# Operands on 64 byte addresses, one transfer for the Toeplitz matrices, and another fill in the state space stage

## The chip, the cores and the metric

The kernel runs on one core of a Trainium2 chip. The metric is device time in microseconds (us) of one execution, as the median of several. The kernel before takes 1503.35 us, median of 3 runs from 1501.92 to 1510.48.

## The reference

Two transformer blocks run one after the other on 512 tokens of width 1024, in float32. The change touches only a part of the first block, the state space branch (S5), and around it the order in which the projections of that block are worked off.

```python
h = rmsnorm(x, norm_mix_pre[l])
proj = h @ w_in[l]
q, k, v, u, g_attn, g_ssm = jnp.split(proj, splits, axis=-1)
y_attn = sliding_window_attention(q, k, v, sinks[l], rel_bias) @ w_attn_branch[l]
z = jax.nn.gelu(s5_ssm(u, ...))
...
# s5_ssm: 32 groups of 16 channels, one complex diagonal state of 64 entries each
mag = jnp.exp(lr * dt)
ab = mag * (cos(li * dt) + i sin(li * dt))
bb = (ab - 1) / lam * b              # discretized input matrix
h_t = ab * h_(t-1) + bb @ u_t        # along the 512 tokens
y_t = re(c @ h_t) + d_skip * u_t
```

Behind it come the gated merge, the output projection and an MLP, and then the second block (a gated linear recurrence in two directions, attention with a band, a gated feed-forward part).

## The kernel before, in words

Every large matrix product is done in three products of a split operand: `xh*wh`, `xl*wh` and `xh*wl`, where `h` is the operand rounded to the fast float32 form and `l` the rest (`mm3`, lines 217 to 219 of the profile). A weight tile `raw`, 128 x 1024, comes in by a DMA issued by SyncE (L190); ScalarE rounds it to `wh` (L202) and VectorE takes the difference `wl` (L203).

The state space branch is computed in chunks of 8 tokens, 64 chunks (`NCH`). `ssm_prep` makes the constants: from `lam` it takes `mag`, sine and cosine (`sincos`), the powers `pw` of the diagonal state matrix, the tables `ph` of the rotations (products of `un`, the sines and cosines of doubled angles), and the input matrix `bb`. All this is small work of VectorE, 32 to 512 elements wide, in the first 60 us beside the projection that makes `u`.

`ssm_quarter` is a generator that does 8 of the 32 groups (a quarter) in five steps:

1. `rotations` (four products and two sums 128x512 on VectorE), and `combine` for `X` and `L1`, the operands that carry a chunk's input into the state and the state into the output. The load of `U` (the inputs) and the zeros for `kscr` are issued.
2. `xTp`: eight transposes of `X`, copied out by ScalarE into `B8`.
3. `kps`: matmuls of 16 columns and 112 columns with `c0` and `L1`; the result `kev` holds the kernel of a chunk. It is written to the DRAM scratch `kscr` behind a strip of zeros, and read back shifted into `dr`, so that each partition has one row of a Toeplitz matrix. ScalarE copies it in another order of its axes into `D8`, the tile that the profile calls D.
4. `pv`: states of each chunk, two copies of halves between partitions by ScalarE (the tiles `g`), a scan along the chunks, and the products with `rot`.
5. `py`: eight pairs of matmuls, `U` with D8 (the profile's `px` of L789) and `rot` with `L1` (L790), and the result's transfer to DRAM.

TensorE's program order is written by hand. In the state space stage a string `SSM` sets it: `qN` advances quarter N by one step, a number gives so many units of fill, each one `mm3`. The fill (`Feed`) is the projections of k, v and q and then the gates; what it doesn't use up is used in the attention that follows (`G1` and `GZ` say how many of them stand where). The order on the other engines is set by a scheduler, which sees the program and its own times.

The pool of tiles on the left side of the SBUF starts with constants. A tile `even` of 4 bytes per partition in it moves the addresses of what comes after it.

Of the kernel before, what the change touches and what calls it, by code (L numbers as in the profile page):

```python
# [9 lines left out]
F32 = mybir.dt.float32  # L10
# [8 lines left out]
P = 128  # L19
T = 512  # L20
# [36 lines left out]
G1 = 19  # L57
# [23 lines left out]
SSM = 'q0 20 q0 q1 12 q0 3 q0 12 q0 q1 q2 10 q1 3 q1 12 q1 q2 q3 10 q2 3 q2 12 q2 q3 8 q3 3 q3 12 q3'  # L81
# [7 lines left out]
L1E = 0  # L89
# [6 lines left out]
GZ = 4  # L96
# [9 lines left out]
def bc(ap, axis, n):  # L106
    dims = [list(d) for d in ap.ap]
    dims.insert(axis, [0, n])
    return bass.AP(ap.tensor, ap.offset, dims)
# [40 lines left out]
class Net:  # L150
    def __init__(self, tc, a, out, ctx):
        self.tc, self.nc, self.a, self.out, self.ctx = tc, tc.nc, a, out, ctx
        E = ctx.enter_context
        self.const = E(tc.tile_pool(name="const", bufs=1))
        self.wraw = E(tc.tile_pool(name="wraw", bufs=3))
        self.wsp = E(tc.tile_pool(name="wsp", bufs=3))
        self.xn = E(tc.tile_pool(name="xn", bufs=KD))
        self.tmp = E(tc.tile_pool(name="tmp", bufs=5))
        self.sm = E(tc.tile_pool(name="sm", bufs=3))
        self.stk = E(tc.tile_pool(name="stk", bufs=1))  # L160
        self.pmm = E(tc.tile_pool(name="pmm", bufs=3, space=PSUM))
        self.pmx = E(tc.tile_pool(name="pmx", bufs=1, space=PSUM))
        self.pss = E(tc.tile_pool(name="pss", bufs=2, space=PSUM))
        self.pst = E(tc.tile_pool(name="pst", bufs=2, space=PSUM))
        self.dram = E(tc.tile_pool(name="dram", bufs=1, space=DRAM))

        E(tc.tile_pool(name="edge", bufs=1, side="right")).tile([P, 8], F32, name="edge")
        self.sm.tile([P, 1], F32, name="even", bufs=1)
        self.wmode, self.wn, self.after = ("av",), 0, None
        self.deferred, self.fin = [], {}  # L170
# [363 lines left out]
    def sincos(self, pool, s, c, hs, x, n):  # L534

        v = self.nc.vector
        k, y, y2, hc = [pool.tile([P, n], F32, name=f"sc{i}") for i in range(4)]
# [44 lines left out]
    def ssm_prep(self, sp, tp, lam):  # L582
# [4 lines left out]
        dt, e1, th, mag, em1, sn, cs, hs = (N(x) for x in ("dt", "e1", "th", "mag", "em1", "sn", "cs", "hs"))  # L587
# [4 lines left out]
        self.sincos(tp, sn, cs, hs, th, G)  # L592
# [42 lines left out]
        un = [tp.tile([P, 9, G], F32, name=f"un{i}") for i in range(2)]  # L635
        ua, ub = (tp.tile([P, 2, G, 4], F32, name=x) for x in ("ua", "ub"))
        v.tensor_copy(un[0][:, 0, :], cs)
        v.tensor_scalar(un[1][:, 0, :], sn, self.sgn, -1.0, MUL, MUL)
        for j in range(8):
            x, y = [w[:, j, :] for w in un], [w[:, j + 1, :] for w in un]  # L640
            v.tensor_tensor(ta, x[1], x[1], MUL)
            v.tensor_tensor(tb, x[0], x[0], MUL)
            v.scalar_tensor_tensor(y[1], x[0], 2.0, x[1], MUL, MUL)
            v.tensor_tensor(y[0], tb, ta, SUB)
        gp.memset(self.ph[0][:, :, :, 0:1], 1.0)
        gp.memset(self.ph[1][:, :, :, 0:1], 0.0)
        for j in range(3):
            n = 1 << j
            y = [bc(w[:, 3 + j::3, :], 3, n) for w in un]
            self.cmul(v, [w[:, :, :, n:2 * n] for w in self.ph], [w[:, :, :, 0:n] for w in self.ph], y,  # L650
                      [w[:, :, :, 0:n] for w in (ua, ub)])
# [23 lines left out]
        zt = sp.tile([P, 112], F32, name="zt")  # L675
        gp.memset(zt, 0.0)
        self.kscr = [self.dram.tile([8, 16, 240], F32, name=f"kscr{q}") for q in range(4)]
# [29 lines left out]
    def ssm_quarter(self, sp, q):  # L707
# [7 lines left out]
        nc.sync.dma_start(self.kscr[q].rearrange("g c l -> (g c) l")[:, 0:112], self.zt)  # L715
# [10 lines left out]
        def combine(eng, o, x1, w1, x2, w2, op):  # L726
            for h in range(0, 8, 4):
                hs = slice(h, h + 4)
                t = (self.t() if eng is v else sp.tile([P, T], F32, name="gt")).rearrange("p (g c l) -> p g c l", g=4, c=16)
                eng.tensor_tensor(o[:, hs], chan(x1)[:, hs], w1[:, hs], MUL)  # L730
                eng.tensor_tensor(t, chan(x2)[:, hs], w2[:, hs], MUL)
                eng.tensor_tensor(o[:, hs], o[:, hs], t, op)

        combine(v, X, self.bb[:, gs, :], pws(self.ar, 0), self.bbs[:, gs, :], pws(self.ais, 0), ADD)
        combine((v, gp)[L1E], L1, c12[1], pws(self.ain, 1), c12[0], pws(self.ars, 1), SUB)

# [8 lines left out]
        kev = sp.tile([16, 8, P], F32, tag="kd", name="kev")  # L745
        for g4 in range(0, 8, 4):
# [7 lines left out]
            p3 = ps[0:16, :].rearrange("p (g n) -> p g n", g=4)  # L754
            v.tensor_tensor(kev[:, g4:g4 + 4, 0:16], p3[:, :, 0:16], self.dd[:, 8 * q + g4:8 * q + g4 + 4, :], ADD)
            nc.scalar.copy(kev[:, g4:g4 + 4, 16:P], p3[:, :, 16:P])
        nc.sync.dma_start(self.kscr[q][:, :, 112:240].rearrange("g c l -> c g l"), kev)
        dr = sp.tile([P, 8, P], F32, tag="kd", name="dr")
        for i in range(8):
            nc.sync.dma_start(dr[i:P:8, :, :], self.kscr[q][:, :, i * 16:i * 16 + P].rearrange("g c l -> c g l"))  # L760
        D8 = sp.tile([P, 8, 16, 8], F32, name="D8", bufs=DB)
        nc.scalar.copy(D8.rearrange("p g c j -> p g j c"), dr.rearrange("p g (j c) -> p g j c", j=8))
# [923 lines left out]
```

## Time and profile before

| what | value |
| --- | --- |
| median of 3 runs | 1503.35 us |
| the profiled execution | 1509.53 us |
| its span | 1507.8 us |
| TensorE busy (PE) | 1446.4 us, 96% |
| VectorE busy (DVE) | 954.2 us, 63% |
| ScalarE busy (ACT) | 667.8 us, 44% |
| GpSimd busy (POOL) | 225.8 us, 15% |
| DMA traffic | 162.03 MB, 107 GB/s on average |

A busy time is the sum of an engine's instructions, without the time in which it waits. TensorE's matmuls overlap, and their ends are modelled. The granted clock (PEclk) is the share of TensorE's full clock that it was given; 0.50 is the lower of its two levels. A timeline gives a start and a duration for each instruction; the spacing of starts tells what an instruction costs in a row of them, since the durations overlap. The stages meant here are the start (to about 57 us), the state space stage (57 to 204), and the attention of the first block with what follows it.

### The profile page before, as it was taken

How to read it: one execution, taken by the hardware profiler on the slowest of the kernel's cores; microseconds unless marked ns; L12 is line 12 of the kernel's file. 1: busy time of each engine (PE TensorE's matmuls, PEld its weight loads, DVE VectorE, ACT ScalarE, POOL GpSimd, SP SyncE). 2: the span in 40 equal slices, each digit the busy share in tenths (PEclk: the TensorE clock that was granted, in tenths of full speed). 3: DMA queues.
4: the chain of work that ended last, by engine and by line, in shares of the span. 5: the costliest groups of instructions: out<-in, count | busy, mean ns of one | idle time of the engine just before them, and what ended most of it. 6: DMA issues, size and time to landing. Idle time of an engine off the chain costs nothing.

```text
span 1507.8 us, 18510 instructions
## 1 busy us (share of the span) xinstructions
PE 1446.4 (96%) x6844; PEld 1191.8 (79%) x6844; DVE 954.2 (63%) x1676; ACT 667.8 (44%) x1102; POOL 225.8 (15%) x183
## 2 busy tenths in 40 slices
PE   8978999899999999999999998999999999999998
PEld 6667778679888888888988776888778888888886
DVE  7986368774743243434879998889764555535534
ACT  6333356535543331322478774667544332312213
POOL 0000000033300000001544462112021111101101
PEclk9978899989999999999999998999999999999999
DMA  7744356243233333333364322331333333233321
GB/s 207 229 117 118 107 150 203 64 147 105 71 98 93 90 97 98 98 97 86 109 176 108 102 70 77 92 84 57 118 93 98 98 98 98 98 98 88 102 91 70
DMA packets 257750, 162.03 MB, mean 107 GB/s; under 512 B 26691, under 2 KB 236028, under 8 KB 257660
## 3 DMA queue, kind: packets, MB, share of 16 engines
q1 hardware_dynamic: 257356, 160.83, 36.4%
q8 instruction: 54, 0.88, 0.2%
q14 instruction: 36, 0.29, 0.1%
q10 hardware_dynamic: 304, 0.02, 0.0%
HBM read 136.74 MB, written 14.65 MB: 100 GB/s over the span
## 4 chain that ended last, share of the span: by engine, by line
PE 76%; DVE 12%; ACT 4%; DMA 3%; issue 3%; SPq 1%; POOL 1%; ACTq 0%; DVEq 0%; POOLq 0%
PE ps L217 16%; PE ps L218 16%; PE ps L219 16%; PE gu L217 5%; PE gu L219 5%; PE gu L218 5%; DVE wl L203 2%; PE lg L847 2%; PE pT L866 1%; SPq L760 1%; PE px L217 1%; PE px L219 1%; PE px L218 1%; PE kps L752 1%; PE px L790 1%
## 5 line engine op out<-in xcount | busy, mean ns | idle before, releaser
L202 ACT CAST wh<-raw 128x1024 fp32r<-128x1024 f32 x216 | 226.0, 1050 | 500.2 <-PE ps L218 255.6
L203 DVE TENSOR_TENSOR wl<-raw,wh 128x1024 fp32r<-128x1024 f32 x216 | 300.3, 1391 | 131.1 <-ACT wh L202 131.0
L217 PE MATMUL ps<-xh,wh 128*128 128x512 f32 (+1 forms) x792 | 317.0, 400 | 0.0
L219 PE MATMUL ps<-xh,wl 128*128 128x512 f32 (+1 forms) x792 | 310.2, 392 | 4.7 <-DVE wl L203 4.7
L218 PE MATMUL ps<-xl,wh 128*128 128x512 f32 (+1 forms) x792 | 310.2, 392 | 1.1 <-DVE xl L186 1.0
L219 PEld LDWEIGHTS ps<-xh,wl 128*128 128x128 f32 x792 | 151.1, 191 | 37.6 <-DVE wl L203 6.0
L218 PEld LDWEIGHTS ps<-xl,wh 128*128 128x128 f32 x792 | 151.6, 191 | 27.6 <-DVE xl L186 2.2
L217 PEld LDWEIGHTS ps<-xh,wh 128*128 128x128 f32 x792 | 151.8, 192 | 27.2 <-issue 2.1
L217 PE MATMUL gu<-xh,wh 128*128 128x512 f32 x352 | 137.4, 390 | 0.0
L219 PE MATMUL gu<-xh,wl 128*128 128x512 f32 x352 | 137.1, 390 | 0.0
L218 PE MATMUL gu<-xl,wh 128*128 128x512 f32 x352 | 137.1, 389 | 0.0
L356 POOL TENSOR_TENSOR acc<-acc,sq 128x256 f32<-128x256 f32 (+1 forms) x46 | 49.4, 1076 | 391.7 <-ACT sq L354 391.0
L217 PE MATMUL ps<-hh,wh 128*128 128x512 f32 (+1 forms) x264 | 100.8, 382 | 0.0
L219 PE MATMUL ps<-hh,wl 128*128 128x512 f32 (+1 forms) x264 | 100.7, 381 | 0.0
L218 PE MATMUL ps<-hl,wh 128*128 128x512 f32 (+1 forms) x264 | 100.6, 381 | 0.0
L219 PEld LDWEIGHTS gu<-xh,wl 128*128 128x128 f32 x352 | 66.1, 188 | 13.8
L218 PEld LDWEIGHTS gu<-xl,wh 128*128 128x128 f32 x352 | 66.1, 188 | 13.6
L217 PEld LDWEIGHTS gu<-xh,wh 128*128 128x128 f32 x352 | 66.1, 188 | 13.5
L1167 DVE SCALAR_TENSOR_TENSOR tw<-ps,rsb 128x512 f32<-128x512 f32 x31 | 21.4, 692 | 77.2 <-PE ps L219 75.8
L1548 POOL TENSOR_TENSOR tw<-tw 128x512 f32<-128x512 f32 x22 | 29.0, 1319 | 255.7 <-ACT wh L202 217.4
L1191 DVE TENSOR_TENSOR f<-f,ps 128x512 f32<-128x512 f32 (+1 forms) x25 | 16.1, 645 | 67.1 <-PE ps L219 67.0
L852 ACT ACTIVATE S<-S,at 128x256 f32<-128x256 f32 (+2 forms) x96 | 50.2, 525 | 18.8 <-DVE at L850 18.7
(451 smaller groups left out, 2724.3 us busy)
## 6 DMA issues: line engine op xcount, KB each, us to landing
raw<-in_w_in SPq DMA_DIRECT2D x70, 512.0 KB, 4.0
raw<-in_w_ffn_in SPq DMA_DIRECT2D x44, 512.0 KB, 3.7
raw<-in_w_ff_in SPq DMA_DIRECT2D x32, 512.0 KB, 3.9
raw<-in_w_ff_out SPq DMA_DIRECT2D x32, 512.0 KB, 3.8
raw<-in_w_ffn_out SPq DMA_DIRECT2D x22, 512.0 KB, 3.5
raw<-in_w_out SPq DMA_DIRECT2D x16, 512.0 KB, 3.7
tscr<-tg SPq DMA_DIRECT2D x16, 256.0 KB, 2.2
tg<-tscr SPq DMA_DIRECT2D x16, 256.0 KB, 3.5
```

The lines of the kernel that those rows point to most:

```text
L202: (nc.scalar.copy if mode[0] == "a" else nc.gpsimd.tensor_copy)(h, raw)
L203: (nc.vector if mode[1] == "v" else nc.gpsimd).tensor_sub(l, raw, h.bitcast(F32))
L217: mm(ps, lhsT=lh, rhs=rh, start=start, stop=False)
L218: mm(ps, lhsT=lh, rhs=rl, start=False, stop=False)
L219: mm(ps, lhsT=ll, rhs=rh, start=False, stop=stop)
L356: nc.gpsimd.tensor_add(self.acc[:, cs], self.acc[:, cs], s[:, cs])
L752: nc.tensor.matmul(ps[0:16, o + 16:o + P].rearrange("p (j c) -> p j c", c=16), lhsT=lb, rhs=L1[:, g, :, 0:7].rearrange("p c j -> p j c"), ...
L847: mm(o, lhsT=q[i][:, qs], rhs=k[j][:, ks], start=j == 0, stop=j == 1)
L852: nc.scalar.activation(S[i // 2][:, i % 2, :], S[i // 2][:, i % 2, :], AF.Exp, bias=nm[:, i:i + 1], accum_out=den[:, i:i + 1])
L1167: v.scalar_tensor_tensor(t, ps, 0.0, rsb, MAX, MUL)
L1191: v.tensor_add(fm, fm, ps[:, cs])
L1548: nc.gpsimd.tensor_tensor(u_, u_, g_, MUL)
```

## The change

The first operand's tile `even` goes, so that the tiles of that side lie on multiples of 64 bytes instead of 32 bytes above one. Sine and cosine are taken for seven angles at once, the angle and its multiples by 8, 16, 32, 64, 128 and 256, 224 elements wide, and the loop of doublings of `un` goes. `combine` does its three products for all eight groups at once. `kev` has its groups innermost: ScalarE copies four groups at once, and VectorE adds `dd` in one instruction instead of two. The scratch `kscr` has one row of 1920 elements per channel, zeros in the first 896, and one transfer with overlapping rows of 4 KB reads it into `dr` where eight transfers did. The copy to `D8` reads with steps and writes in a row. The string `SSM` and the two numbers `G1` and `GZ` are others.

```diff
@@ -54,7 +54,7 @@
 WU = 'ag'.split(",")
 
 UL = 2
-G1 = 19
+G1 = 16
 NS1 = 2
 NT1 = 2
 R1 = 48
@@ -78,7 +78,7 @@
 H3 = 12
 H1 = 9
 LRU = '10 c0 c1 7 g0 c2 15 g1 u3 c3 13 g2 5 u4 c4 g3 u5 9 c5 g4 u6 c6 10 g5 0 u7 c7 10 g6 21 g7'
-SSM = 'q0 20 q0 q1 12 q0 3 q0 12 q0 q1 q2 10 q1 3 q1 12 q1 q2 q3 10 q2 3 q2 12 q2 q3 8 q3 3 q3 12 q3'
+SSM = 'q0 20 q0 13 q0 1 q0 9 q1 9 q0 q1 8 q1 3 q1 q2 14 q1 q2 7 q2 3 q2 6 q3 7 q2 q3 4 q3 3 q3 14 q3'
 DB = 1
 WX = 3
 WD = 18
@@ -86,14 +86,13 @@
 WE = 5
 UC = 3
 WK = 7
-L1E = 0
 SG = 0
 OB = 0
 NE1 = 4
 NE = 5
 ZJ = 2
 NP = 5
-GZ = 4
+GZ = 5
 X1 = 3
 X2 = 6
 EW = 1
@@ -165,7 +164,6 @@
         self.dram = E(tc.tile_pool(name="dram", bufs=1, space=DRAM))
 
         E(tc.tile_pool(name="edge", bufs=1, side="right")).tile([P, 8], F32, name="edge")
-        self.sm.tile([P, 1], F32, name="even", bufs=1)
         self.wmode, self.wn, self.after = ("av",), 0, None
         self.deferred, self.fin = [], {}
 
@@ -534,7 +532,7 @@
     def sincos(self, pool, s, c, hs, x, n):
 
         v = self.nc.vector
-        k, y, y2, hc = [pool.tile([P, n], F32, name=f"sc{i}") for i in range(4)]
+        k, y, y2, hc = [pool.tile(n, F32, name=f"sc{i}") for i in range(4)]
         c1 = 6.28125
         c2 = float(np.float32(np.round((2 * math.pi - c1) * 2 ** 20) / 2 ** 20))
         c3 = float(np.float32(2 * math.pi - c1 - c2))
@@ -584,12 +582,18 @@
         G = 32
         lr, li = lam[:, 0, :], lam[:, 1, :]
         N = lambda nm: tp.tile([P, G], F32, name=nm)
-        dt, e1, th, mag, em1, sn, cs, hs = (N(x) for x in ("dt", "e1", "th", "mag", "em1", "sn", "cs", "hs"))
+        dt, e1, th, mag, em1 = (N(x) for x in ("dt", "e1", "th", "mag", "em1"))
         self.exp_exact(tp, dt, lam[:, 2, :], G)
         v.tensor_tensor(e1, lr, dt, MUL)
         v.tensor_tensor(th, li, dt, MUL)
         self.exp_exact(tp, mag, e1, G, em1)
-        self.sincos(tp, sn, cs, hs, th, G)
+        sn, cs, hs, th7 = (tp.tile([P, 7, G], F32, name=x) for x in ("sn", "cs", "hs", "th7"))
+        for i, j in enumerate((0, 3, 4, 5, 6, 7, 8)):
+            v.tensor_scalar(th7[:, i, :], th, float(1 << j), None, MUL)
+        self.sincos(tp, sn, cs, hs, th7, [P, 7, G])
+        un = [cs[:, 1:, :], tp.tile([P, 6, G], F32, name="un")]
+        v.tensor_scalar(un[1], sn[:, 1:, :], self.sgn, -1.0, MUL, MUL)
+        sn, cs, hs = (x[:, 0, :] for x in (sn, cs, hs))
         pw = [sp.tile([P, G, 9], F32, name=f"pw{i}") for i in range(2)]
         t2 = [tp.tile([P, G, 4], F32, name=f"pt{i}") for i in range(2)]
         v.memset(pw[0][:, :, 0:1], 1.0)
@@ -632,21 +636,12 @@
         self.dec = sp.tile([P, 8, NCH], F32, name="dec")
         gp.memset(self.dec[:, :, 0:1], 0.0)
         self.ph = [sp.tile([P, 2, G, 8], F32, name=f"ph{i}") for i in range(2)]
-        un = [tp.tile([P, 9, G], F32, name=f"un{i}") for i in range(2)]
         ua, ub = (tp.tile([P, 2, G, 4], F32, name=x) for x in ("ua", "ub"))
-        v.tensor_copy(un[0][:, 0, :], cs)
-        v.tensor_scalar(un[1][:, 0, :], sn, self.sgn, -1.0, MUL, MUL)
-        for j in range(8):
-            x, y = [w[:, j, :] for w in un], [w[:, j + 1, :] for w in un]
-            v.tensor_tensor(ta, x[1], x[1], MUL)
-            v.tensor_tensor(tb, x[0], x[0], MUL)
-            v.scalar_tensor_tensor(y[1], x[0], 2.0, x[1], MUL, MUL)
-            v.tensor_tensor(y[0], tb, ta, SUB)
         gp.memset(self.ph[0][:, :, :, 0:1], 1.0)
         gp.memset(self.ph[1][:, :, :, 0:1], 0.0)
         for j in range(3):
             n = 1 << j
-            y = [bc(w[:, 3 + j::3, :], 3, n) for w in un]
+            y = [bc(w[:, j::3, :], 3, n) for w in un]
             self.cmul(v, [w[:, :, :, n:2 * n] for w in self.ph], [w[:, :, :, 0:n] for w in self.ph], y,
                       [w[:, :, :, 0:n] for w in (ua, ub)])
 
@@ -672,9 +667,9 @@
         self.dd = sp.tile([16, G, 16], F32, name="dd")
         with self.tc.issue_after(self.after):
             gp.tensor_tensor(self.dd, bc(self.ident[0:16, 0:16], 1, G), bc(dsk[:, :], 2, 16), MUL)
-        zt = sp.tile([P, 112], F32, name="zt")
+        zt = sp.tile([16, 112 * 8], F32, name="zt")
         gp.memset(zt, 0.0)
-        self.kscr = [self.dram.tile([8, 16, 240], F32, name=f"kscr{q}") for q in range(4)]
+        self.kscr = [self.dram.tile([16, 240 * 8], F32, name=f"kscr{q}") for q in range(4)]
         self.yscr = [self.dram.tile([8, 16, T], F32, name=f"yscr{q}") for q in range(4)]
         self.zt = zt
 
@@ -712,7 +707,7 @@
         c12, c0 = [self.c12[:, i, gs, :] for i in range(2)], self.c0[:, gs, :]
         U = sp.tile([P, 8, NCH], F32, name="U", bufs=UU)
         nc.sync.dma_start(U, self.uscr[q].rearrange("g c (i m) -> (c i) g m", i=8))
-        nc.sync.dma_start(self.kscr[q].rearrange("g c l -> (g c) l")[:, 0:112], self.zt)
+        nc.sync.dma_start(self.kscr[q][:, 0:112 * 8], self.zt)
 
         def pws(w, l0):
             return bc(w[:, gs, l0:l0 + 8], 2, 16)
@@ -723,16 +718,14 @@
         X = sp.tile([P, 8, 16, 8], F32, name="X")
         L1 = sp.tile([P, 8, 16, 8], F32, name="L1", bufs=MB)
 
-        def combine(eng, o, x1, w1, x2, w2, op):
-            for h in range(0, 8, 4):
-                hs = slice(h, h + 4)
-                t = (self.t() if eng is v else sp.tile([P, T], F32, name="gt")).rearrange("p (g c l) -> p g c l", g=4, c=16)
-                eng.tensor_tensor(o[:, hs], chan(x1)[:, hs], w1[:, hs], MUL)
-                eng.tensor_tensor(t, chan(x2)[:, hs], w2[:, hs], MUL)
-                eng.tensor_tensor(o[:, hs], o[:, hs], t, op)
-
-        combine(v, X, self.bb[:, gs, :], pws(self.ar, 0), self.bbs[:, gs, :], pws(self.ais, 0), ADD)
-        combine((v, gp)[L1E], L1, c12[1], pws(self.ain, 1), c12[0], pws(self.ars, 1), SUB)
+        def combine(o, x1, w1, x2, w2, op):
+            t = sp.tile([P, 8, 16, 8], F32, name="ct")
+            v.tensor_tensor(o, chan(x1), w1, MUL)
+            v.tensor_tensor(t, chan(x2), w2, MUL)
+            v.tensor_tensor(o, o, t, op)
+
+        combine(X, self.bb[:, gs, :], pws(self.ar, 0), self.bbs[:, gs, :], pws(self.ais, 0), ADD)
+        combine(L1, c12[1], pws(self.ain, 1), c12[0], pws(self.ars, 1), SUB)
 
         yield
         B8 = sp.tile([P, 8, P], F32, name="B8")
@@ -742,7 +735,7 @@
                 nc.tensor.transpose(ps[:, g * P:(g + 1) * P], X[:, g4 + g].rearrange("p c i -> p (c i)"), self.ident)
             nc.scalar.copy(B8[:, g4:g4 + 4, :], ps.rearrange("p (g n) -> p g n", g=4))
         yield
-        kev = sp.tile([16, 8, P], F32, tag="kd", name="kev")
+        kev = sp.tile([16, P, 8], F32, tag="kd", name="kev")
         for g4 in range(0, 8, 4):
             ps = self.pst.tile([P, T], F32, tag="t", name="kps")
             for g in range(g4, g4 + 4):
@@ -751,15 +744,14 @@
                 nc.tensor.matmul(ps[0:16, o:o + 16], lhsT=lb, rhs=c0[:, g, :], start=True, stop=True)
                 nc.tensor.matmul(ps[0:16, o + 16:o + P].rearrange("p (j c) -> p j c", c=16), lhsT=lb,
                                  rhs=L1[:, g, :, 0:7].rearrange("p c j -> p j c"), start=True, stop=True)
-            p3 = ps[0:16, :].rearrange("p (g n) -> p g n", g=4)
-            v.tensor_tensor(kev[:, g4:g4 + 4, 0:16], p3[:, :, 0:16], self.dd[:, 8 * q + g4:8 * q + g4 + 4, :], ADD)
-            nc.scalar.copy(kev[:, g4:g4 + 4, 16:P], p3[:, :, 16:P])
-        nc.sync.dma_start(self.kscr[q][:, :, 112:240].rearrange("g c l -> c g l"), kev)
-        dr = sp.tile([P, 8, P], F32, tag="kd", name="dr")
-        for i in range(8):
-            nc.sync.dma_start(dr[i:P:8, :, :], self.kscr[q][:, :, i * 16:i * 16 + P].rearrange("g c l -> c g l"))
+            nc.scalar.copy(kev[:, :, g4:g4 + 4].rearrange("p l g -> p g l"), ps[0:16, :].rearrange("p (g l) -> p g l", g=4))
+        v.tensor_tensor(kev[:, 0:16, :], kev[:, 0:16, :], self.dd[:, gs, :].rearrange("p g c -> p c g"), ADD)
+        nc.sync.dma_start(self.kscr[q][:, 112 * 8:], kev.rearrange("p l g -> p (l g)"))
+        dr = sp.tile([P, P, 8], F32, tag="kd", name="dr")
+        k = self.kscr[q][:, :]
+        nc.sync.dma_start(dr.rearrange("p l g -> p (l g)"), bass.AP(k.tensor, k.offset, [[1920, 16], [128, 8], [1, 1024]]))
         D8 = sp.tile([P, 8, 16, 8], F32, name="D8", bufs=DB)
-        nc.scalar.copy(D8.rearrange("p g c j -> p g j c"), dr.rearrange("p g (j c) -> p g j c", j=8))
+        nc.scalar.copy(D8, dr.rearrange("p (j c) g -> p g c j", j=8))
         yield
 
 
```

The first place is on VectorE, ahead of the last instruction of the first quarter's `X`, on which its `xTp` waits. `un`, `ta` and `tb` are of the doublings, `wl` is of a weight, `ct` is a product for `combine`, `ph` and `rot` are of the rotations, `sc` is a scaled projection result. Before:

```order
L730 TENSOR_TENSOR X<-bb,pw_481 128x512 x2
L730 TENSOR_TENSOR L_729<-c_648,ain 128x512 x2
L730 TENSOR_TENSOR L_870<-c_648,ain 128x512 x2
L957 TENSOR_TENSOR sc<-ps,rsb 128x512
L641 TENSOR_TENSOR ta<-un_544 128x32
L642 TENSOR_TENSOR tb<-un_543 128x32
L643 SCALAR_TENSOR_TENSOR un_544<-un_543,un_544 128x32
L203 TENSOR_TENSOR wl<-raw,wh 128x1024
L732 TENSOR_TENSOR X<-X,tw 128x512 x2
L732 TENSOR_TENSOR L_729<-L_729,tw 128x512 x2
L644 TENSOR_TENSOR un_543<-tb,ta 128x32
L564 TENSOR_TENSOR ub<-ph_542,un_544 128x64
```

After:

```order
L201 TENSOR_TENSOR wl<-raw,wh 128x1024
L566 TENSOR_TENSOR pw_491<-pt_492,pt_493 128x32x4
L562 TENSOR_TENSOR rt_691<-ph_551 128x512
L627 TENSOR_SCALAR ais<-pw_491,sgn 128x288
L629 TENSOR_SCALAR ain<-pw_491 128x288
L563 TENSOR_TENSOR rot_688<-rt_690,rt_691 128x512
L724 TENSOR_TENSOR ct<-bbs,ais 128x1024
L723 TENSOR_TENSOR L_702<-c_621,ain 128x1024
L723 TENSOR_TENSOR L_1012<-c_621,ain 128x1024
L564 TENSOR_TENSOR rt_690<-ph_550,ph_551 128x512
L565 TENSOR_TENSOR rt_691<-ph_551,ph_550 128x512
L725 TENSOR_TENSOR X<-X,ct 128x1024
```

In before the first `rot` tiles stood behind `X`; now four of their products, and two instructions of `ph` and `pw`, stand ahead of the last instruction of `X`, and `X`'s products are 1024 wide.

The second place is on SyncE, which issues the transfers in order, at the second quarter: `raw` is a weight, `tscr<-tg` a result of the gates. Before:

```order
L190 DMA raw<-in_w_in 128x8x128
L757 DMA kscr_623<-kev 16x8x128
L760 DMA dr<-kscr_623 16x8x128 x8
L503 DMA tscr<-tg 128x512
L190 DMA raw<-in_w_in 128x8x128
L503 DMA tscr<-tg 128x512
```

After:

```order
L188 DMA raw<-in_w_in 128x8x128
L749 DMA kscr_596<-kev 16x1024
L752 DMA dr<-kscr_596 128x1x1024
L501 DMA tscr<-tg 128x512
L188 DMA raw<-in_w_in 128x8x128
L501 DMA tscr<-tg 128x512
```

Eight issues that read `dr` are one; the neighbours are the same.

The third is on ScalarE, in the same quarter: `kev` is the evacuation of `kps`, `D` the Toeplitz copy, `g` the copies between halves, `tg` a gate's tanh. Before:

```order
L771 COPY g_1260<-pv 64x512
L772 COPY g_1260<-pv 64x512
L756 COPY kev<-kps 16x4x112 x2
L202 CAST wh<-raw 128x1024
L502 ACTIVATE tg<-tg 128x512
L779 COPY g_1259<-g_1260 64x512
L780 COPY g_1259<-g_1260 64x512
L770 COPY dec<-mag_537 128x8x63
L202 CAST wh<-raw 128x1024
L502 ACTIVATE tg<-tg 128x512
L762 COPY D_1239<-dr 128x8x8x16
```

After:

```order
L747 COPY kev<-kps 16x4x128 x2
L763 COPY g_1179<-pv 64x512
L764 COPY g_1179<-pv 64x512
L200 CAST wh<-raw 128x1024
L500 ACTIVATE tg<-tg 128x512
L754 COPY D_1158<-dr 128x1024
L771 COPY g_1178<-g_1179 64x512
L772 COPY g_1178<-g_1179 64x512
```

`kev` has moved ahead of the first pair of `g` copies, and `D` ahead of the second pair.

## Rows read from the trace of the kernel before

**Rows 1.** Windows by stage: from:to, length, busy us (instructions) per engine, PEclk, DMA, GB/s.

```profile
7.00:57.00 50.00, 49.32 (x224) 39.77 (x225) 48.68 (x178) 29.11 (x47) 3.09 (x2) 1.00 0.85 258
57.00:103.00 46.00, 34.77 (x175) 28.06 (x174) 37.61 (x77) 12.91 (x18) 0.00 (x0) 0.82 0.50 128
```

**Rows 2.** Waits of TensorE, 56 to 204 us: total us, times, longest.

```profile
PE px L789 <- ACT D L762: 11.2, 3, 5.9
PE px L790 <- DVE rot L782: 4.3, 2, 2.2
PE kps L751 <- ACT kev L756: 2.1, 1, 2.1
```

**Rows 3.** The windows view again, four stretches at the lower clock.

```profile
73.10:76.40 3.30, 3.30 (x12) 2.33 (x11) 2.34 (x9) 1.00 (x2) 0.00 (x0) 0.50 0.55 139
90.20:107.10 16.90, 11.79 (x47) 10.99 (x48) 10.09 (x17) 7.23 (x9) 0.00 (x0) 0.50 0.58 143
131.20:144.60 13.40, 11.05 (x46) 10.57 (x47) 3.92 (x7) 3.78 (x4) 0.00 (x0) 0.50 0.53 146
168.70:178.80 10.10, 10.04 (x43) 9.65 (x44) 1.23 (x2) 2.43 (x5) 0.00 (x0) 0.50 0.36 105
```

**Rows 4.** Timeline of TensorE: start us, us, engine, line, operation.

```profile
46.27 0.39 PE L217 MATMUL ps<-xh,wh 128*128 128x512 f32 x1
46.50 0.39 PE L218 MATMUL ps<-xl,wh 128*128 128x512 f32 x1
...
56.70 1.17 PE L742 MATMUL xTp<-ident,X 128*128 128x128 f32 x8
```

**Rows 5.** Timeline of VectorE, three places.

```profile
18.34 0.19 DVE L551 SCALAR_TENSOR_TENSOR hs<-hs,sc 128x32 f32<-128x32 f32 x1
18.45 0.19 DVE L555 SCALAR_TENSOR_TENSOR sc<-sc,sc 128x32 f32<-128x32 f32 x1
...
54.72 1.23 DVE L203 TENSOR_TENSOR wl<-raw,wh 128x1024 fp32r<-128x1024 f32 x1
55.85 1.30 DVE L732 TENSOR_TENSOR X<-X,tw 128x512 f32<-128x512 f32 x2
...
74.97 0.42 DVE L563 TENSOR_TENSOR ua<-ph,un 128x256 f32<-128x256 f32 x1
75.31 0.42 DVE L564 TENSOR_TENSOR ub<-ph,un 128x256 f32<-128x256 f32 x1
```

**Rows 6.** The chain of waits in a quarter, 120 to 135 us: start, us, what.

```profile
122.52 2.01 DMA kscr<-kev
...
124.55 0.59 SPq L760
...
129.03 2.27 DMA dr<-kscr
```

**Rows 7.** DMA issues, 57 to 204 us: count, KB each, median us to landing.

```profile
raw<-in_w_in SPq DMA_DIRECT2D x12, 512.0 KB, 3.8
...
U<-uscr SPq DMA_DIRECT2D x2, 256.0 KB, 3.0
```

**Rows 8.** Groups by line, ScalarE, 57 to 204 us: busy us, mean ns, idle before.

```profile
L202 ACT CAST wh<-raw 128x1024 fp32r<-128x1024 f32 x13 | 13.7, 1053 | 25.3 <-PE ps L218 23.2 <-issue 2.1
L762 ACT COPY D<-dr 128x1024 f32<-128x1024 f32 x4 | 8.4, 2111 | 4.6 <-DMA dr<-kscr 4.6
...
L756 ACT COPY kev<-kps 16x448 f32<-16x448 f32 x8 | 4.1, 521 | 10.0 <-DVE kev L755 10.0
```

**Rows 9.** The same view: VectorE from 39 us on, TensorE 57 to 204.

```profile
L510 DVE TENSOR_TENSOR su<-ps,rsb 128x512 f32<-128x512 f32 x3 | 3.2, 1132 | 0.0
...
L768 PE MATMUL pv<-U,B 128*128 128x64 f32 x64 | 7.6, 272 | 0.0
```

**Rows 10.** The same view of TensorE from 312 us on.

```profile
L219 PE MATMUL ps<-xh,wl 128*128 128x512 f32 x560 | 221.1, 395 | 4.7 <-DVE wl L203 4.7
...
L218 PE MATMUL ps<-wl,hh 128*128 128x512 f32 x132 | 52.3, 396 | 0.1
```

## The prediction

> **What bounds the kernel now.** I read first the windows by stage, then the waits of TensorE (PE), then the granted clock, and only then single instructions. From 7 to 57 us VectorE (DVE) is busy 48.7 of 50 us [rows 1]: in this stretch it carries the splits of the weights and the constants of the state space branch, and PE is fed at its pace. From 57 us to about 200 us the four quarters of the state space branch run between units of projection work (a unit is three 128x512 matmuls). Here PE sets the end and its program order is fixed, so whatever PE waits for is lost. The waits are few [rows 2]: 11.2 us for the tile D (the Toeplitz matrices, copied by ScalarE) in three quarters, 4.3 for the rotated states `rot` in two, 2.1 for kev. [...]
>
> A unit at full clock is three matmul starts 0.23 apart [rows 4], 0.68 us.
>
> **The start: sine and cosine at seven angles.** The chain of eight doublings (four 128x32 instructions each) goes; sine and cosine are computed for seven multiples at once, so 25 instructions of sincos become 224 wide. DVE takes its queue in order, and the order after puts most of this ahead of X, the operand of the first transposes xTp. In before X was just in time: PE began xTp at 56.70 without a wait [rows 4], while DVE ran the last X instructions from 55.85 to 57.15 [rows 5]. Counting what stands ahead of the last X instruction in both orders: 23 fewer 128x32 products of three operands and 20 fewer other 32 wide ones, at 0.10 each (the starts of the 32 wide rows at 18.34 and 18.45 [rows 5]), -4.3; 26 more 192 or 224 wide (the 25 and a scaling), at 0.30 (between 0.10 for 32 and 0.34 for 256 wide, nearer the latter [rows 5]), +7.8; six more 64 wide, six 128 wide and six 256 wide (the products for ph, which before stood behind X) at 0.14, 0.20 and 0.34, +4.1; five more 1024 wide at 1.13 [rows 5], +5.7, and three fewer 512 wide at 0.60 (half of X's pair), -1.8. Together +11.5; where the narrow ones run beside waits of the same queue it is less, down to 6, and the most is 12. PE has nothing else: the 28 units ahead of xTp are the same, and it comes to xTp at about 57. So it waits 11 us, until about 68, and then, as after every wait of this kind in before, is busy about 10 us at half clock [rows 3], another 5. **Term A: +16** (9 to 18).
>
> **The quarters: the chain from kps to py.** Before, in the quarter that the chain shows, kscr<-kev takes 2.01 us, then SyncE issues eight transfers one behind the other (0.59 each from 124.55 on, 4.5 in all), and the last lands 2.27 after its issue [rows 6]; then D is copied, 2.11 us [rows 8]. From kps on that is kev 1.0 (two at 521 ns [rows 8]) + 2.0 + 4.5 + 2.3 + 2.1 = 11.9, and with ScalarE's two copies of g ahead of kev, at 0.6 like other 512 wide work, 13.1. The cover was 15 units and pv, 15 x 0.68 = 10.2 and 1.9 (a quarter of pv's 7.6 [rows 9]): 12.1. So D was late.
>
> After: one issue, no chain of eight. The one transfer is 512 KB in rows of 4 KB; the trace has no such read of an overlapping scratch row. The nearest are raw, 512 KB at 3.8, and U, 256 KB at 3.0 [rows 7]; for the upper end I take three times raw's, 12, since raw loads stand ahead of it in the same queue; for the lower the last small piece's 2.3. I take 3.9. kev is now written with a step of 32 bytes. Strided copies cost double in rows: D, 1024 wide, takes 2111 ns where the plain wh of that width takes 1053 [rows 8], and su, 512 wide and read with steps, 1132 [rows 9] against 0.65 for each 512 wide instruction of X's pair [rows 5]; so kev goes from 521 [rows 8] to about 1.05 a copy, bounded by 0.52 and 1.2. D's copy is still strided on one side: 2.1, bounded by 1.05 and 2.2. The path after the second kps: 1.05 + 0.2 (the narrow addition of dd, now one) + 2.0 + 3.9 + 2.1 = 9.3. In the order after, D stands ahead of the second pair of g copies, so rot is ready at 9.3 + 1.2 (two copies) + 1.4 (two products, 512 wide, at 0.60 to 0.69) = about 12. The new fill covers 17, 16 and 17 units and pv in quarters 1 to 3: 13.5, 12.8 and 13.5 us. Both fit, with about 1 us to spare for rot and 3.5 to 4.2 for D.
>
> [...]
>
> In the first quarter xTp0 and py0 have 32 units between them instead of 27, 3.4 us more cover, its transfers lose the same 3 us, and kps no longer waits for an addition on DVE ahead of ScalarE's copy. The longest wait for D, 5.9 [rows 2], goes. DVE's backlog is 11 us longer, but PE comes 11 us later as well. **Term B, the first quarter:** waits 5.9 + 2.1 (rot, half of 4.3) + 2.1 (kev) = 10.1, and clock (3.30 + 11.79)/2 = 7.5: -17.6. **Term C, the others:** D 11.2 - 5.9 = 5.3, rot 2.2, clock (11.05 + 10.04)/2 = 10.5: -18.0.
>
> **The rest, at nothing.** The removed "even" tile puts most operands at multiples of 64 bytes instead of 32 above one. Before already has matmuls of both kinds: hh lay 32 above, xh and wl on the multiple, and they take 396 and 395 ns [rows 10]. One ns on 6844 matmuls would be 7 us either way; as the rows show either kind at the same duration, I take 0. The zero strips are off every path (issued at each quarter's start). combine is the same work in half as many instructions, counted above. GZ and G1 move units from the attention stage into this one and back; the count of units does not change.
>
> **Sum:** 16.0 - 17.6 - 18.0 = -19.6 on the profiled execution of 1509.5 us, which lies 6.2 above the median 1503.35. On the median: **1484 us**.
>
> **The rivals.** *X is not late* (0.14): the wide sincos runs in gaps that I don't see, and A is zero. DVE's 1.3 idle us of 50 [rows 1] speak against, the doublings' dependences (each waits for the one before) for it. 1484 - 16 = 1468. *The quarters keep waiting* (0.26): 1 us to spare is thin; if rot or D comes 2.5 us later than reckoned in quarters 1 to 3, waits of about 2 each return and with them the low clock, 10.5: C shrinks from -18.0 to about -1.5, 1500; if in one of the three only, 1489. *The one transfer lands late* (0.09), the slower side: eight partitions' rows read the same scratch, behind raw loads in one queue. Each us beyond about 5 costs one in each of three quarters, and the low clock stays as it was; beyond 9 the first quarter waits too. With a landing of t us the sum is 16 - 17.6 + 3(t - 5) - 7.5, so from t = 8 the kernel is slower than before; at 12, with some 3 us and 7 of clock in the first quarter, 1525. raw's 3.8 speaks against. *Alignment matters after all* (0.05), by up to 7 us either way beside the rest. The forecast as worked out has 0.46, and with it a range of its own of 1476 to 1492 (A between 9 and 18, D's and kev's ends).
>
> **How the numbers follow.** A measurement of this kernel tells no change from about 0.5%, 7.5 us: 1495.8 to 1510.9. Forecast, X not late and alignment are faster (0.64 of 0.65), of the quarters' rival half is faster (0.13) and half the same, of the late transfer 0.07 is slower. That gives 0.77, 0.14 and 0.09. The range 1466 to 1501 takes in the first three cases but for their ends.
>
> **What would show it.** Right: a wait of about 11 us of xTp0 for DVE's X near 57, and a low clock behind it; no waits of PE for D or rot in quarters 1 to 3, and a clock of 1.00 from 80 to 185 us; dr in one issue, landing in about 3.9; kev at about 1.05, D still at 2.1; the stage up to 204 shorter by about 20, everything behind it the same. Wrong: no wait at xTp0; D or rot still named in the waits; dr landing above 8.

## The result and the profile after

The changed kernel takes 1484.1 us (median of 4, 1480.72 to 1485.31), the kernel before in the same job 1504.27: ratio 0.9856, 95% interval 0.9822 to 0.989, 20.2 us less. The profiled executions lie further apart, with spans of 1478.9 and 1507.8, because that of before was above its median and that of after below; the comparisons below go by medians.

The windows by stage after, with the same columns as [rows 1], and one more stretch, the one at the lower clock:

```profile
57.00:103.00 46.00, 35.19 (x187) 28.74 (x187) 40.41 (x53) 15.43 (x19) 0.00 (x0) 0.85 0.46 128
103.00:204.00 101.00, 99.15 (x569) 80.31 (x569) 67.08 (x94) 53.98 (x78) 0.00 (x0) 1.00 0.50 144
60.00:72.70 12.70, 5.03 (x16) 4.39 (x17) 12.70 (x18) 1.17 (x2) 0.00 (x0) 0.50 0.43 124
73.00:204.00 131.00, 129.01 (x738) 104.46 (x737) 91.49 (x126) 68.24 (x95) 0.00 (x0) 1.00 0.50 141
```

From 73 to 204 us TensorE is busy 129 of 131 us at full clock; the four low stretches of [rows 3] have become one, from 60 to 72.7, in which PE was busy 5.03 us. In windows of 1 us from 50 to 320 us the kernel before and the changed kernel show a granted clock of 1.00 or 0.50, and a value between the two only where a change lies inside the window. Matmuls of 512 columns start 0.43 us apart in the low stretch (70.26 to 72.82) and 0.23 behind it (74.05 to 75.89). PE's waits after, for [rows 2]:

```profile
PE xTp L735 <- DVE X L725: 11.4, 1, 11.4
...
PE px L782 <- DVE rot L774: 0.5, 1, 0.5
```

All waits for D and kev are gone, and of those for rot 0.5 is left. In their place stands the wait that was forecast, at the first xTp. The timelines of TensorE and of VectorE there (for [rows 4] and [rows 5]) show what it waited for:

```profile
67.67 1.08 PE L735 MATMUL xTp<-ident,X 128*128 128x128 f32 x4 [11.39 <-DVE X L725]
```

```profile
65.11 0.67 DVE L564 TENSOR_TENSOR rt<-ph,ph 128x512 f32<-128x512 f32 x1
65.71 0.67 DVE L565 TENSOR_TENSOR rt<-ph,ph 128x512 f32<-128x512 f32 x1
66.31 1.21 DVE L725 TENSOR_TENSOR X<-X,ct 128x1024 f32<-128x1024 f32 x1
```

The last instruction of X starts at 66.31 instead of 55.85, with two products for rot right ahead of it. The transfer and ScalarE's copies, for [rows 7] and [rows 8]:

```profile
raw<-in_w_in SPq DMA_DIRECT2D x14, 512.0 KB, 4.1
...
dr<-kscr SPq DMA_DIRECT2D x4, 512.0 KB, 4.9
```

```profile
L747 ACT COPY kev<-kps 16x512 f32<-16x512 f32 x8 | 9.0, 1120 | 9.4 <-PE kps L745 7.1 <-DMA tscr<-tg 2.3
L754 ACT COPY D<-dr 128x1024 f32<-128x1024 f32 x4 | 8.5, 2122 | 7.7 <-DMA dr<-kscr 7.7
```

The transfer lands in 4.9 (forecast 3.9), kev takes 1120 ns a copy (1.05), D 2122 (2.1). So far the trace follows the forecast line by line. What it does not show is which edit did it; the experiments do.

One more row differs, in a part that the change leaves alone in the order. The groups of TensorE behind 310 us, for [rows 10]:

```profile
L217 PE MATMUL ps<-xh,wl 128*128 128x512 f32 x560 | 219.8, 393 | 6.2 <-DVE wl L201 6.2
...
L217 PE MATMUL gu<-xh,wl 128*128 128x512 f32 x352 | 137.0, 389 | 0.0
...
L216 PE MATMUL ps<-wl,hh 128*128 128x512 f32 x132 | 51.5, 390 | 0.3 <-DVE wl L201 0.3
```

The matmuls with hh take 390 ns instead of 396. The group of xh with wl, which the prediction held beside them, is a mean over full and low clock (393 here, 395 before; in before the clock was 0.50 from 878.7 to 885.4 us, and four of these matmuls took 671 ns there). The group gu, which in before runs from 1135 to 1422 us at a clock of 1.00 throughout, took 390 there already, and that was the row to compare with:

```profile
L219 PE MATMUL gu<-xh,wl 128*128 128x512 f32 x352 | 137.1, 390 | 0.0
```

### The profile page after: what moved, and what is told of

Same layout as the page of the kernel before. It is cut to its first block, busy times and chain, and to the rows that moved or that the text cites. A ratio compares the mean times of both kernels' runs of the same rounds, so it can differ in the third digit from the quotient of the medians.

```text
span 1478.9 us, 18427 instructions
## 1 busy us (share of the span) xinstructions
PE 1420.8 (96%) x6844; PEld 1178.2 (80%) x6844; DVE 954.3 (65%) x1622; ACT 671.5 (45%) x1102; POOL 225.8 (15%) x183
## 4 chain that ended last, share of the span: by engine, by line
PE 73%; DVE 11%; ACT 4%; issue 3%; DMA 1%; POOL 1%; SPq 0%; ACTq 0%; DVEq 0%; POOLq 0%
PE ps L215 16%; PE ps L216 16%; PE ps L217 15%; PE gu L215 5%; PE gu L216 5%; PE gu L217 5%; DVE wl L201 2%; PE lg L839 1%; PE pT L858 1%; PE px L215 1%; PE px L217 1%; PE px L216 1%; PE px L870 1%; PE px L871 1%; PE kps L745 1%
```

## The experiments

Twelve kernels, each timed 4 to 12 times beside the kernel before. Ratios are to it, with 95% intervals, and allow for the kernel before having come out at 1504.2 to 1505.6 us from job to job; the text calls the kernels by the number at the start of their label.

| label | kernel | median us | ratio |
| --- | --- | --- | --- |
| | changed | 1484.1 | 0.9856 [0.9822, 0.989] |
| e1_chain | changed, doublings back | 1483.74 | 0.9855 [0.9834, 0.9876] |
| e2_oldfill | changed, old fill | 1500.53 | 0.9963 [0.9949, 0.9978] |
| e3_newfill | before, new fill | 1508.26 | 1.0015 [1.0, 1.0029] |
| e4_dr1 | before, transfer part | 1505.74 | 0.9998 [0.9984, 1.0012] |
| e5_noeven | before, no 4 byte tile | 1496.97 | 0.9946 [0.9927, 0.9965] |
| e6_even | changed, 4 byte tile back | 1491.77 | 0.9914 [0.9898, 0.993] |
| e7_dr1_newfill | before, transfer part and new fill | 1509.64 | 1.0033 [1.0021, 1.0046] |
| e8_pool | changed, doublings back, work on GpSimd | 1491.61 | 0.991 [0.9894, 0.9926] |
| e9_half | changed, combine of before | 1501.12 | 0.9973 [0.9961, 0.9986] |
| e10_dr8 | changed, dr in eight transfers | 1483.15 | 0.9859 [0.984, 0.9878] |
| e11_fill | changed, more fill ahead of xTp | 1493.15 | 0.9925 [0.9909, 0.994] |
| e12_fillcomb | before, no 4 byte tile, new fill, new combine | 1483.91 | 0.9848 [0.9824, 0.9871] |

**The doublings back in the changed kernel.**

```diff
-        sn, cs, hs, th7 = (tp.tile([P, 7, G], F32, name=x) ...)
-        self.sincos(tp, sn, cs, hs, th7, [P, 7, G])
+        self.sincos(tp, sn, cs, hs, th, [P, G])
+        for j in range(8):   # the four instructions of a doubling
```

> The changed kernel with one part undone: the eight doublings of sine and cosine are back, sincos is 32 wide again; all else as changed. Theory (VectorE's queue ahead of X is 11 us longer and nothing else makes X late): TensorE no longer waits at the first xTp, no low clock behind it, and the kernel takes 16 us less than the changed one, 1468 (1464 to 1473). Rival (X is late because combine is now in 1024 wide pieces, or for the rotations that were moved ahead): a wait of 5 us or more stays at xTp, 1475 to 1484. Second rival (the rotations, now later, become the wait at the first py): the wait at xTp goes, but 5 to 10 us come back at py0, 1475 to 1480.

The time did not move. PE's waits in it:

```profile
PE px L786 <- DVE rot L778: 9.2, 2, 8.7
...
PE xTp L739 <- DVE X L729: 0.8, 1, 0.8
```

The second rival has the mechanism, though not the time (1475 to 1480): the wait at xTp falls from 11.4 to 0.8, and 8.7 of a new wait for rot stands at the first py, with the clock low (0.50) from 73 to 84 and 97 to 111 us. The first product with rot starts at 102.26 in e1 and at 99.81 in the changed kernel:

```profile
102.26 0.69 PE L786 MATMUL px<-rot,L 128*128 128x63 f32 x2 [8.70 <-DVE rot L778]
```

```profile
99.81 0.43 PE L782 MATMUL px<-rot,L 128*128 128x63 f32 x2
```

So VectorE's queue up to the first rot ends at about the same time in both, and the wide sincos only chooses whether it holds up PE at xTp or at py. VectorE is not simply full there: between 57 and 100 us in e1 it is busy 35.7 of 43 us, and most of the rest is one wait in its queue, for a weight that ScalarE rounds.

```profile
86.10 1.23 DVE L201 TENSOR_TENSOR wl<-raw,wh 128x1024 fp32r<-128x1024 f32 x1 [5.30 <-ACT wh L200]
```

What another order of that queue would give was not run.

**The old fill in the changed kernel**, and **the new fill alone** and **the transfer part alone** in the kernel before:

```diff
-SSM = 'q0 20 q0 13 q0 1 q0 9 q1 9 q0 q1 8 ...'    # e2; e3 the other way round
+SSM = 'q0 20 q0 q1 12 q0 3 q0 12 q0 q1 q2 10 ...'
-    nc.sync.dma_start(dr[i:P:8, :, :], ...)       # e4: eight become one
+    nc.sync.dma_start(dr..., bass.AP(k.tensor, k.offset, [[1920, 16], [128, 8], [1, 1024]]))
```

> The changed kernel with the fill of before (the string and the two numbers); the one transfer, the wide sincos and the rest stay. Theory (the shorter chain by itself does most of it): after the second kps D is ready in 9 to 10 us and rot in 12, the old fill covers 12.1, so waits of at most 1 us a quarter, in one or two of them a low clock of 5; 1484 to 1493. Rival (the fill does it, the transfer hardly): the waits for D come back at 2 to 5 us a quarter, low clock in three, 1498 or more.

> The kernel before with the new fill alone (the string and the two numbers); eight transfers, kev and the doublings as before. Theory (both are needed): D needs 13.1 us after kps and the new fill covers 12.8 to 13.5, so D is late by 0 to 2 in some quarters, and in the first quarter 2 to 3 of its 5.9 stay, with low clock there; X is in time as before; 1482 to 1493. Rival (fill alone is enough): no waits for D behind the first quarter, 1470 to 1480. Rival (fill does nothing): 1498 or more.

> The kernel before with the transfer part alone (kev with the groups innermost, scratch rows of 1920, one transfer for dr, D's copy); fill, doublings, combine and the 4 byte tile as before. Theory: the waits for D in the second to fourth quarters go and those of the first shrink to 1 or 2 us, X is in time, so it lies 10 to 16 under the same with the wide sincos: 1470 to 1480. Rival (one transfer lands no earlier than the eight): 1498 to 1508.

All three theories missed, and the rivals that gave 1498 or more have the numbers, though not all of their reasons. With the old fill the changed kernel loses 16.4 us, and waits for rot and D come back (e2):

```profile
PE px L782 <- DVE rot L774: 8.1, 4, 2.3
PE px L781 <- ACT D L754: 4.5, 2, 4.0
```

So the fill is needed; but the new fill alone (e3) gives nothing, and the transfer part alone (e4) gives nothing. The waits of e4:

```profile
PE px L789 <- DVE rot L781: 17.9, 3, 14.0
...
PE px L788 <- ACT D L761: 0.8, 1, 0.8
```

D is in time (0.8 left of 11.2), as forecast, and rot has taken its place: 17.9, of which 14.0 at one py. Removing the wait for one of py's two operands gained nothing, because the other came later.

**Alignment alone.**

```diff
-        self.sm.tile([P, 1], F32, name="even", bufs=1)    # e5; e6 puts it back
```

> The kernel before without its 4 byte tile, nothing else: most tiles now lie on multiples of 64 bytes. Theory (a matmul whose moving operand lies 32 bytes above a multiple of 64 starts 6 to 8 ns later than one on the multiple: 0.233 to 0.235 against 0.227 between starts of the matmuls with hh, hl and mh in the trace of before and of the changed kernel): the time behind 433 us shrinks by 10 us, the stages ahead of it stay; 1505.6 - 10 = 1495.5 (1493.5 to 1497.5). Rival (the 10 us between the two traces behind 433 us are of something else, as the prediction had it): 1502 to 1508.

> The changed kernel with the 4 byte tile put back, nothing else. Theory (alignment is worth 10 us, the rest of the change the other 11.5): 1494 (1492 to 1496), starts of the matmuls with hh 0.233 to 0.235 apart again, the first 433 us as in the changed kernel. Rival (alignment is worth nothing): 1482 to 1486.

Both theories hold, with 8 us instead of 10, and e6 lies 0.2 below its range: e5 is 8.1 us faster than the kernel before (by the ratio, 5.3 to 11), and e6 7.7 slower than the changed kernel (by the medians). The same group without the tile, in e5, and with it, in e6:

```profile
L218 PE MATMUL ps<-hh,wl 128*128 128x512 f32 x232 | 90.2, 389 | 0.0
```

```profile
L218 PE MATMUL ps<-hh,wl 128*128 128x512 f32 x232 | 91.6, 395 | 0.0
```

389 against 395 ns. The ends of matmuls are modelled, but starts say the same: in a row of these groups they lie 0.227 us apart in the changed kernel (559.68 to 562.86 us) and 0.233 in the kernel before (560.19 to 562.99). There are three such groups of 232 and three of 132 with wl or wh and hh or hl: 1092 matmuls by 6 ns are 6.6 of the 8 us. The groups with hh or hl that write px and those with mh or ml, some 370 matmuls, fell by 3 to 7 ns too; with them the estimate comes to about 8.

**Transfer and fill together in the kernel before.**

> The kernel before with the transfer part and the new fill together; doublings, combine and the 4 byte tile as before. Theory (each of the two alone gave nothing, because the other limit stands behind it; together they take away the waits for D and rot in the second to fourth quarters, and the wide sincos adds or takes nothing, since VectorE's queue up to the first rot is as long either way): 1494 (1490 to 1498), with a wait for rot at the first py of some 9 us instead of one at the first xTp. Rival (the wide sincos is needed, as it brings the first rot forward): 1500 to 1506.

Neither: 5 us slower than before, with waits for rot in three quarters.

```profile
PE px L789 <- DVE rot L781: 15.7, 3, 6.6
```

Beside e1 this is the telling miss, since the two kernels differ, beside the tile, in combine alone, and lie 26 us apart, of which the tile explains 8.

**Work of the later quarters on GpSimd.**

```diff
+        self.cmul(self.nc.gpsimd if q else self.nc.vector, rot, hi, lo, tt)
+        combine(gp if q else v, L1, ...)              # with the doublings back
```

> The changed kernel with the eight doublings back, and the rotations and L1 of quarters 2 to 4 on GpSimd, idle in this stage, instead of VectorE. Theory (VectorE's queue up to the first rot is the bound of the stretch to 100 us, whether it shows at xTp or at py): some 8 us of second quarter work leave the queue ahead of the first rot, the 9.2 us wait for rot in the kernel with the doublings shrinks to about 1 and the low clock behind it goes: 1470 (1466 to 1476). Rival (GpSimd at more than twice VectorE's time, or the two engines slowing each other, makes L1 or rot of the later quarters late): a wait at kps or px appears there, 1482 or more.

The rival has the time and the second of its two reasons, but most of the wait is not where it put it: of 13.2 us of waits for rot, 10.5 stand at the first py. VectorE beside a running GpSimd:

```profile
44.58 2.73 POOL L729 TENSOR_TENSOR L<-L,gt 128x1024 f32<-128x1024 f32 x1
44.97 2.38 DVE L643 TENSOR_TENSOR un<-tb,ta 128x32 f32<-128x32 f32 x1
```

```profile
92.20 1.55 DVE L770 TENSOR_TENSOR g<-g,rot 128x512 f32<-128x512 f32 x1
...
95.35 1.55 DVE L771 TENSOR_TENSOR g<-g,g 128x512 f32<-128x512 f32 x1
```

The 128x32 instruction, which takes 0.18 in e1, took 2.38 and ended with the GpSimd instruction beside it (47.35 and 47.31), and 512 wide products took 1.55 instead of the 0.68 and 0.69 of e1, in a stretch (86.5 to 98 us) in which GpSimd was busy 10.93 of 11.5 us. GpSimd's idle time was no free capacity.

**combine undone in the changed kernel.**

```diff
-            t = sp.tile([P, 8, 16, 8], F32, name="ct")
+            for h in range(0, 8, 4):
+                t = (self.t() if eng is v else ...)...   # self.t(): the shared scratch tile tw, 512 wide
```

> The changed kernel with combine undone: its products again in halves of 512, with the rotating scratch tile tw that other work shares; all else as changed. Theory (the own scratch tile lets the next quarter's combine run ahead; with the shared one, VectorE has six to nine of its instructions between this quarter's products and its scan, and rot comes 5 us later in the second and third quarters, as in the kernel with transfer and fill on the kernel before): waits for rot of 3 to 5 us in two or three quarters and low clock behind them; 1496 (1491 to 1503). Rival (combine costs the same in halves, as the prediction had it): 1482 to 1487.

The theory holds: 17 us slower, nearly the whole gain. VectorE in the second quarter, with combine undone:

```profile
118.04 0.37 DVE L750 TENSOR_TENSOR kev<-kev,dd 16x128 f32<-16x128 f32 x1 [4.39 <-ACT kev L749]
121.59 0.69 DVE L499 TENSOR_TENSOR tg<-ps,rsb 128x512 f32<-128x512 f32 x1 [3.17 <-PE ps L217]
...
122.79 0.68 DVE L768 TENSOR_TENSOR g<-g,rot 128x512 f32<-128x512 f32 x1
123.39 1.29 DVE L726 TENSOR_TENSOR tw<-bbs,ais 128x512 f32<-128x512 f32 x2
124.60 0.68 DVE L726 TENSOR_TENSOR tw<-c,ars 128x512 f32<-128x512 f32 x1
...
126.34 0.68 DVE L769 TENSOR_TENSOR g<-g,g 128x512 f32<-128x512 f32 x1
126.94 1.28 DVE L727 TENSOR_TENSOR X<-X,tw 128x512 f32<-128x512 f32 x2
...
129.34 1.21 DVE L771 TENSOR_TENSOR_SCAN g<-dec,g 128x512 f32<-128x512 f32 x1
...
134.00 0.68 DVE L776 TENSOR_TENSOR rot<-rot,rot 128x512 f32<-128x512 f32 x1
```

and in the changed kernel:

```profile
119.48 0.68 DVE L766 TENSOR_TENSOR g<-g,rot 128x512 f32<-128x512 f32 x1
...
121.21 0.69 DVE L767 TENSOR_TENSOR g<-g,g 128x512 f32<-128x512 f32 x1
121.93 1.23 DVE L769 TENSOR_TENSOR_SCAN g<-dec,g 128x512 f32<-128x512 f32 x1
...
125.85 0.69 DVE L774 TENSOR_TENSOR rot<-rot,rot 128x512 f32<-128x512 f32 x1
```

From the second product of g to rot it is 11.2 us in the one and 6.4 in the other. With the shared tile the next quarter's combine (tw, X, L) stands between the products of g and the scan; with its own tile it has run before. It is the order and not the amount of work: in e9 VectorE stood idle 4.39 and 3.17 us just ahead of this stretch. The waits:

```profile
PE xTp L737 <- DVE X L727: 11.2, 1, 11.2
PE px L784 <- DVE rot L776: 10.6, 4, 4.8
```

10.6 us for rot, with low clock (0.50) at 102 to 109, 133 to 143 and 167 to 181 us. Whether it is the own tile or the width of 1024 that moves combine was not separated. e9 is only some 4 us faster than the kernel before although it keeps the alignment, worth 8: without the new combine the rest of the change costs about 4, much as in e7.

**Eight transfers again in the changed kernel**, and **more fill ahead of the first xTp**:

```diff
+            for i in range(8):                                         # e10
+                nc.sync.dma_start(dr[i:P:8]..., k[:, i * 128:i * 128 + 1024])
-SSM = 'q0 20 q0 13 ...'                                                # e11, GZ 5 to 7
+SSM = 'q0 34 q0 13 ...'
```

> The changed kernel with dr read by eight transfers of 64 KB again (rows of 4 KB, so the layout stays), everything else as changed; the other engines' order is the same. Theory (eight issues and the last landing, 4.5 + 2.3, are 2 us longer than the one transfer's 4.9, and D has 3 to 4 us to spare): D comes 2 to 3 us later, rot, behind D on ScalarE, 1 to 2 us late in two or three quarters: 1486 (1483 to 1492). Rival (the one transfer is what carries the gain): D waits of 3 us and more in each quarter, 1494 or more. Rival (nothing at all): 1482 to 1485.

> The changed kernel with 14 more units of fill ahead of the first xTp (34 instead of 20 in the string, GZ 7 so that there are units enough; the attention behind it has that many fewer). Theory (the 11.4 us wait at the first xTp is TensorE out of work while VectorE works; the two weights more cost VectorE 2.3 us ahead of X): the wait shrinks to 3 to 5 us, the clock stays up or falls for less, 8 to 13 us are gained there, and the attention, short of 14 units at its end, gives back some: 1478 (1472 to 1484). Rival (the attention gives it all back, since PE's work is the same and its waits only move): 1484 to 1490.

The eight transfers cost nothing that can be measured (1483.15), as the last rival had it: the waits for D that come back are small.

```profile
PE px L782 <- ACT D L755: 2.5, 3, 1.0
```

More fill ahead of xTp shrinks that wait to 2.9, about as forecast, but PE waits 5.6 for rot, and the attention, with 14 units fewer, waits for ScalarE and VectorE (18.9 us from 204 to 320 us, 10.0 in the changed kernel) and runs at low clock (0.50) in five short stretches between 246 and 309 us: 9 us slower than the changed kernel. The rival was right in sign and too small.

**Three edits on the kernel before.**

```diff
-        self.sm.tile([P, 1], F32, name="even", bufs=1)
+SSM = 'q0 20 q0 13 q0 1 q0 9 q1 9 q0 q1 8 ...'      # G1 16, GZ 5
+            t = sp.tile([P, 8, 16, 8], F32, name="ct")   # combine as changed
```

> The kernel before with three parts of the change: no 4 byte tile, the new fill, and combine in pieces of 1024 with its own scratch tile. The transfer part (kev, scratch, eight transfers, D's copy) and the doublings stay as before. Theory (alignment 8 to 9 us, and fill and combine together the other 12; the one transfer and the wide sincos carry nothing): 1484 (1480 to 1489), with a wait for rot of some 9 us at the first py in place of the one at the first xTp. Rival (kev and the transfer are needed too: D is ready 13 us after kps at cover 12.8 to 13.5): waits for D of 1 to 3 us in the quarters with low clock behind them, 1490 to 1500.

1483.91: the whole gain, with eight transfers of 64 KB, the old kev and the doublings. Its waits:

```profile
PE px L786 <- ACT D L759: 7.6, 2, 7.3
PE kps L748 <- ACT kev L753: 1.8, 1, 1.8
PE xTp L739 <- DVE X L729: 1.5, 1, 1.5
```

A wait at the first py came, 7.3 where some 9 were forecast, but for D, not for rot; only 0.3 of the 7.6 stands in the later quarters.

## Why the prediction was right in size, and where it was wrong

**The time** (1484 forecast, 1484.1 measured) and the sign are right, and in the trace after the waits go and come where each step said. The causes behind the sum are partly wrong, and that it came out to the microsecond is luck: two errors cancelled.

**Term A** (+16) was right as a place and a size: 11.4 us of wait and half of 5.03 us of busy time at low clock, 13.9 (that stretch was forecast twice as long). It was wrong as a term to be added. e1 takes it away and gains nothing, because VectorE's queue up to the first rot is a bound of its own, which then shows at py. The claim that the rival "X is not late" would give 1468 falls with it.

**Terms B and C** (-35.6) rested on waits of one execution, and on half of PE's busy time at a clock of 0.50 [rows 3] as lost (by the starts in the changed kernel, 0.43 us apart against 0.23, it is 0.47). The same order without the tile, profiled in e5, has 10.1, 4.2 and 2.2 us of these waits and 25.66 us of busy time at low clock, half of it taken as lost, 29.3 in all; one low stretch of [rows 3] is missing in it:

```profile
PE px L788 <- ACT D L761: 10.1, 3, 4.9
PE px L789 <- DVE rot L781: 4.2, 2, 2.2
PE kps L750 <- ACT kev L755: 2.2, 1, 2.2
```

```profile
73.20:79.70 6.50, 6.00 (x26) 4.27 (x27) 5.44 (x20) 1.44 (x3) 0.00 (x0) 0.50 0.35 91
94.00:106.50 12.50, 9.66 (x42) 9.33 (x43) 6.32 (x11) 4.86 (x8) 0.00 (x0) 0.50 0.60 152
135.00:145.00 10.00, 10.00 (x44) 9.57 (x44) 3.67 (x7) 1.76 (x3) 0.00 (x0) 0.51 0.44 118
```

29.3 less the 14.4 that the changed kernel still loses (13.9, and 0.5 for rot) is 14.9; measured are 12.9 (e5 against the changed kernel) and 12.5 (e6 against before). So the stage gave 13 and not 19.6. The missing stretch, 168.7 to 178.8, is worth 5.0, half of its busy 10.04: the prediction counted its losses on an execution 6.2 us above the median and took them off the median, which supposes that none of the 6.2 lay in this stage. That the stretch is missing in a median execution of before is likely from this, but not shown, since before has one trace.

**What earned it** was told wrongly. The prediction gave the gain to the shorter chain through the one transfer and to the fill, and put combine among the edits at nothing ("the same work in half as many instructions"). e10 and e12 show that the one transfer carries nothing measurable, e1 and e12 the same of the wide sincos, e9 that combine carries 17 in company with the fill, e2 that the fill carries 16 in company with combine, and e3, e4 and e7 that fill and transfer without the new combine carry nothing. The step that failed is combine's price of nothing, and with it the path to rot: combine was counted by its work and not by its place in VectorE's queue, and the path counted two copies and two products and took for granted that the queue held little else between them. In the changed kernel that holds, and so the waits came out; it holds because of the new combine. With before's form of combine six instructions of the next quarter stand there, and two more behind the scan, as e9 shows; the prediction read the order at three places and not at this one.

**"Alignment, at nothing"** failed: 8 us. The rival gave it up to 7 with a chance of 0.05. The mistake was in the choice of rows: a group averaged over clocks of 1.00 and 0.50 beside one that ran at 1.00 alone.

The 6.6 us by which stage and sum differ and the 8 of alignment nearly cancel; that is why the number is right. The chances at the end of the prediction do not add up either: by its own parts they are 0.77, 0.16 and 0.07.

**kev, D, the transfer:** durations as forecast, within 1 us for the transfer and 0.1 for the copies; no wait of PE in this stage names the zero strips.

## What to carry to other kernels

When an operation waits for two operands, price the later of the two after the edit, and read in the order of the producing engine everything that stands between the producer's inputs and its result. Work of the next stage can stand there: here combine in wide pieces with a scratch tile of its own, which ran earlier, was worth 17 us in company with the fill, and one transfer instead of eight nothing. Before adding terms, ask whether two of them are one backlog that shows at two places: if so, only the longer counts.

## What was not expected of the hardware

A matmul of 512 columns whose operand lay 32 bytes above a multiple of 64 took 395 to 396 ns instead of 389 to 390, in both directions of the edit (e5, e6). Only this one offset was run, so which multiple counts is not shown. While GpSimd worked on tiles in SBUF (e8), VectorE's products of two tiles in SBUF took 1.55 us instead of 0.68, and a short one 2.38 instead of 0.18, ending with the GpSimd instruction beside it.
